# A two-layer decoder trunk: expert weights fetched in 8192-byte packets, one expert's extra columns put behind a branch, products paired

## The chip, the cores and the metric

The kernel runs on one core of one Trainium2 chip. The metric is device time in microseconds (us) from start to end of one launch. The engines are TensorE (PE: products and transposes), VectorE (DVE), ScalarE (ACT), GpSimd (POOL) and SyncE (SP), and sixteen DMA engines bring data from device memory. Each engine runs its own list of instructions in order, and semaphores tie the lists together.

## The reference, cut to what matters

256 tokens of width 1024, float32, pass two layers; after each half layer comes `x <- LayerNorm(alpha * x + sublayer(x))`.

```python
# layer 0: sliding-window attention with sinks, then a dense SwiGLU (1024 -> 3584 -> 1024)
# layer 1: sparse attention from three branches, gated and added:
kcc = gelu(flat(k blocks + pos_k) @ ck_w1) @ ck_w2     # "compressed"; the same for v
o = g0 * compressed + g1 * selected + g2 * window       # 16 heads, 4 k/v heads, 64 wide
# then the experts
vals, ids = top_k(x @ router, 2); w = softmax(vals)     # 2 of 8 for each token
for e in range(8):
    out += gate[:, e] * ((silu(x @ w_gate[e]) * (x @ w_up[e])) @ w_down[e])
```

Every expert has 3 x 1024 x 3584 float32 weights, 44.04 MB. With the reference's inputs the router gives the eight experts 60, 51, 78, 71, 71, 61, 58 and 62 (token, expert) pairs; expert 0 has 60.

## The kernel before

**Weights.** All weights pass through one planned list (`plan` L145, `plan_later` L151) as tiles of 1 MiB, 128 partitions x 8 KB. `load` (L159) issues them on SP's queue in order (L168) while a buffer is free, and each issue waits until the tile that lay in that buffer before has been used. In the expert stage there are 19 such buffers, under the names `raw`, `more` and `later`. A `w_down` tile holds 256 rows of 1024 numbers: rows 0 to 127 in the first half of each partition's 8 KB, rows 128 to 255 in the second, so a partition is filled from two places of 4 KB. The tiles of `w_gate` and `w_up` are made of pieces of 4 KB too (1024 columns), or of 2 KB for the last 512 of the 3584 columns (`WIDE` is 1024, 1024, 1024, 512).

**Dense part.** Up to the experts each weight is split into two fp32r halves (`hi` by ACT L120, `lo` by DVE L121), and each product is done three times (L204 to L206). The compression of layer 1 uses fp32 weights as they are (L803): 64 positions against 256 columns, first all of k and then all of v. The sparse attention works in units of one or two heads (`unit`, L905): scores, softmax, transposes, and then products with v (L948) that write 64 of the 128 rows of a PSUM bank, head 0 the first 64 and head 1 the others. For the second 128 tokens a unit is one head, so its four products all write the same 64 rows; for the first 128 tokens a unit has both heads, and its products alternate between them.

**Experts.** The eight experts run one after another (`run_experts`, L1162), expert 0 first and the others in an order that the kernel works out from the counts; the jobs have room for 96, 64, 96, 96, 64, 96, 96 and 64 tokens, whatever the counts are, and a leftover pass behind `tc.If(over > 0)` (L1403) takes what does not fit. The first 64 tokens of an expert are the "halves": 64 columns of PE at a time, two groups side by side (L1187 for gate and up, L1210 for down). A job with room for 96 has "quads" too: 32 tokens, four groups side by side (L1195, L1216). Both use the same weight tiles, in an order that alternates (`two`, L1168), and a group of tiles is free for new weights when both have used it. Seven of the eight experts' numbers are read by SP from the tile `whole` (L1381) before it can issue their weights. Those numbers come from the counts (`cnt`, by a product with ones, L1353 on).

The PE's order in the expert stage is the order of the code (`manual_schedule`).

Of the kernel before, what the change touches and what calls it, by code (L numbers as in the profile page):

```python
# [84 lines left out]
def trunk(ctx: ExitStack, tc: tile.TileContext, a, out, dbg=None):  # L85
# [14 lines left out]

    cbf = const.tile([P, 3 * P], BF16, name="cbf")
# [43 lines left out]
    def plan(src, exact=True, pieces=1):  # L145
        kt, cols = src.shape[0] // P, src.shape[1]
        n = max(i for i in range(1, PART // cols + 1) if kt % i == 0)
        for k0 in range(0, kt, n):
            order.append((lambda k0=k0: src[k0 * P:(k0 + n) * P, :], n, cols, exact, pieces))

    def plan_later(src, rows, cols):  # L151
# [3 lines left out]
        for r in range(rows.start, rows.stop, n * P):  # L155
            order.append((lambda r=r: src()[r:r + n * P, cols], n, width, False, 1))

    def load():

        while state["loaded"] < len(order) and len(raws) < state["ahead"]:  # L160
            src, n, cols, exact, pieces = order[state["loaded"]]
# [300 lines left out]
    plan(wa[:, :512], pieces=2)  # L462
# [21 lines left out]
    w1s = [a[w][0, q * 1024:(q + 1) * 1024, :] for w in ("b_cmp_k_w1", "b_cmp_v_w1") for q in range(2)]  # L484
# [11 lines left out]
    def plan_experts(w):  # L496

        back = None
        for wg, wu, wd in w:
            f0 = 0  # L500
            for wide in WIDE:
# [6 lines left out]
                back = wd, f, slice(0, D)  # L508
# [27 lines left out]
    with tc.tile_pool(name="swa", bufs=1) as pool:  # L536
# [53 lines left out]
        with tc.manual_schedule(engines={PE.engine}):  # L590
            for _ in project(Ts, 512, ps_q[0], 2):
                pass
# [148 lines left out]
    zeros = const.tile([P, P], BF16, name="zeros")  # L741
    POOL.memset(zeros, 0.0)
    SP.dma_start(cmask, a["cmask"].rearrange("(t p) k c -> p t k c", p=P))
    with tc.tile_pool(name="nsa", bufs=1) as pool:
# [33 lines left out]
        def compress():  # L778
# [6 lines left out]
            hc = bank().rearrange("p (k h) -> p k h", k=2)[:C]  # L785
# [20 lines left out]
            hx, hy = (pool.tile([P, 2, CMP_HID], F32, name="hx", tag="pt", bufs=PT)[:C] for _ in range(2))  # L806
# [10 lines left out]
            pb = bank().rearrange("p (k j c) -> p k j c", k=4, j=2)[:, :2, :, :]  # L817
            for k in range(2):
                for j in range(2):
                    PE.transpose(pb[:, k, j, :], hx[:, k, j * P:(j + 1) * P], ident[:C, :C])  # L820
# [82 lines left out]
        sums = {}  # L903

        def unit(t, j, heads):  # L905
# [37 lines left out]
            if heads[0] == 0:  # L943
                sums[t, j] = bank()[:, :P]
            po = sums[t, j]
# [123 lines left out]
    class Expert:  # L1069
        def __init__(self, cap, slot_e, gate_e):  # L1070

            self.cap, self.slot, self.gate = cap, slot_e, gate_e
# [89 lines left out]
    def run_experts(jobs):  # L1162
# [3 lines left out]

        state["turn"] = 0

        def two(first, second, between=None):

            steps = [first, second][::-1 if state["turn"] and second else 1]
            if second:
                state["turn"] = 1 - state["turn"]
            steps[0]()
            if between:
# [279 lines left out]
```

## Time and profile before

| | us |
|---|---|
| time, median of 3 runs | 1413.41 (1411.89 to 1418.05) |
| the profiled execution: its time | 1413.78 |
| its span in the trace | 1412.0, mean granted TensorE clock 0.99 |
| TensorE busy (matmuls) | 1360.7 (96%) |
| VectorE, ScalarE, GpSimd busy | 442.0, 342.4, 8.4 |
| DMA | 434.86 MB, mean 308 GB/s |

The busy share of TensorE hides two stages. Up to about 530 us it is the dense stage, where the DMA engines are used by half or less; from 540 us it is the expert stage, where TensorE and the DMA engines are both at or near full use. The ends of pipelined matmuls are modelled, so a stretch that reads as fully busy may hold short waits.

### The profile page before, as it was taken

How to read it: one execution, taken by the hardware profiler on the slowest of the kernel's cores; microseconds unless marked ns; L12 is line 12 of the kernel's file. 1: busy time of each engine (PE TensorE's matmuls, PEld its weight loads, DVE VectorE, ACT ScalarE, POOL GpSimd, SP SyncE). 2: the span in 40 equal slices, each digit the busy share in tenths (PEclk: the TensorE clock that was granted, in tenths of full speed). 3: DMA queues.
4: the chain of work that ended last, by engine and by line, in shares of the span. 5: the costliest groups of instructions: out<-in, count | busy, mean ns of one | idle time of the engine just before them, and what ended most of it. 6: DMA issues, size and time to landing. Idle time of an engine off the chain costs nothing. (4 is left out here: it accounts for less than half of the span.)

```text
span 1412.0 us, 23279 instructions
## 1 busy us (share of the span) xinstructions
PE 1360.7 (96%) x9761; PEld 784.5 (56%) x9762; DVE 442.0 (31%) x1004; ACT 342.4 (24%) x783; POOL 8.4 (1%) x17
## 2 busy tenths in 40 slices
PE   7999999999999999999999999999998999999984
PEld 6777888887777774453344354444343454445331
DVE  6876544556958753000101001100100100200103
ACT  5754444444456721010001001000101000100100
POOL 0000000000000000000000000000000000000000
PEclk9999999999999998999999999999999999999997
DMA  9516565554372067899999999999999999999994
GB/s 349 181 61 211 181 192 192 179 179 155 122 271 91 31 266 272 345 389 377 409 403 409 407 401 409 408 402 407 408 402 409 408 401 408 408 395 393 408 402 179
DMA packets 143679, 434.86 MB, mean 308 GB/s; under 512 B 11312, under 2 KB 18128, under 8 KB 143568
## 3 DMA queue, kind: packets, MB, share of 16 engines
q1 hardware_dynamic: 138416, 428.85, 79.3%
q10 hardware_dynamic: 5152, 4.45, 1.0%
q8 instruction: 79, 1.29, 0.4%
q14 instruction: 32, 0.26, 0.1%
HBM read 432.23 MB, written 1.05 MB: 307 GB/s over the span
## 5 line engine op out<-in xcount | busy, mean ns | idle before, releaser
L121 DVE TENSOR_TENSOR lo<-raw,hi 128x512 fp32r<-128x512 f32 (+2 forms) x244 | 166.4, 730 | 106.5 <-ACT hi L120 106.3
L1187 PE MATMUL ps<-more,Th 128*64 128x512 f32 (+1 forms) x920 | 186.8, 555 | 5.7 <-DMA more<-in_moe_w_gate 5.4
L120 ACT ACTIVATE hi<-raw 128x512 fp32r<-128x512 f32 (+2 forms) x244 | 146.0, 659 | 142.4 <-PE ps L206 129.5
L204 PE MATMUL ps<-hi,Th 128*128 128x512 f32 (+1 forms) x432 | 171.4, 397 | 4.4 <-ACT hi L120 3.2
L206 PE MATMUL ps<-hi,Tl 128*128 128x512 f32 (+1 forms) x432 | 168.6, 391 | 1.4 <-DVE Tl L121 1.4
L205 PE MATMUL ps<-lo,Th 128*128 128x512 f32 (+1 forms) x432 | 168.3, 390 | 0.0
L1244 DVE TENSOR_TENSOR h<-h,ps 128x512 f32<-128x512 f32 (+1 forms) x32 | 19.9, 621 | 448.4 <-PE ps L1187 448.4
L1187 PE MATMUL ps<-later,Th 128*64 128x512 f32 (+1 forms) x680 | 128.9, 525 | 2.1 <-DMA later<-in_moe_w_gate 1.8
L1187 PEld LDWEIGHTS ps<-more,Th 128*64 128x64 f32 x920 | 65.0, 138 | 115.5 <-issue 98.4
L204 PEld LDWEIGHTS ps<-hi,Th 128*128 128x128 f32 x432 | 81.9, 190 | 23.6 <-ACT hi L120 3.6
L1187 PE MATMUL ps<-raw,Th 128*64 128x512 f32 (+1 forms) x448 | 94.4, 561 | 0.6 <-ACT Th L1095 0.6
L1210 PE MATMUL ps<-more,hTa 128*64 128x512 f32 x408 | 92.2, 595 | 2.7 <-DMA more<-in_moe_w_down 2.7
L1236 ACT ACTIVATE h<-ps 128x512 f32<-128x512 f32 (+1 forms) x32 | 17.4, 544 | 315.1 <-PE ps L1187 315.1
L206 PEld LDWEIGHTS ps<-hi,Tl 128*128 128x128 f32 x432 | 81.8, 189 | 20.4 <-DVE Tl L121 2.9
L205 PEld LDWEIGHTS ps<-lo,Th 128*128 128x128 f32 x432 | 82.0, 190 | 16.8 <-DVE lo L121 0.4
L1187 PEld LDWEIGHTS ps<-later,Th 128*64 128x64 f32 x680 | 47.8, 137 | 72.1 <-issue 60.1
L1210 PE MATMUL ps<-later,hTa 128*64 128x512 f32 x312 | 70.3, 594 | 2.0 <-DMA later<-in_moe_w_down 2.0
L1210 PEld LDWEIGHTS ps<-more,hTa 128*64 128x64 f32 x408 | 28.4, 137 | 60.6 <-issue 54.6
L1187 PEld LDWEIGHTS ps<-raw,Th 128*64 128x64 f32 x448 | 31.7, 139 | 53.1 <-issue 48.6
L1195 PE MATMUL ps<-more,Th 128*32 128x256 f32 (+1 forms) x1136 | 60.2, 359 | 0.0
L1239 ACT ACTIVATE hb<-ps 128x256 f32<-128x256 f32 (+1 forms) x20 | 7.2, 358 | 189.0 <-PE ps L1195 189.0
L1243 DVE TENSOR_TENSOR hb<-hb,ps 128x256 f32<-128x256 f32 (+1 forms) x20 | 7.8, 388 | 142.3 <-PE ps L1195 142.3
(256 smaller groups left out, 1444.5 us busy)
## 6 DMA issues: line engine op xcount, KB each, us to landing
more<-in_moe_w_up SPq DMA_DIRECT2D x53, 1024.0 KB, 18.1
more<-in_moe_w_down SPq DMA_DIRECT2D x51, 1024.0 KB, 18.0
more<-in_moe_w_gate SPq DMA_DIRECT2D x50, 1024.0 KB, 18.2
later<-in_moe_w_down SPq DMA_DIRECT2D x38, 1024.0 KB, 15.1
later<-in_moe_w_gate SPq DMA_DIRECT2D x36, 1024.0 KB, 18.3
later<-in_moe_w_up SPq DMA_DIRECT2D x35, 1024.0 KB, 18.0
raw<-in_moe_w_gate SPq DMA_DIRECT2D x26, 1024.0 KB, 18.0
raw<-in_moe_w_up SPq DMA_DIRECT2D x24, 1024.0 KB, 18.2
```

The costliest lines, as they stand in the source:

```text
L120: state["act"] = ACT.activation(hi, src, AF.Copy)
L121: DVE.tensor_tensor(lo, src, hi.bitcast(F32), op=OP.subtract)
L204: PE.matmul(ps, xh, wh, start=first, stop=False)
L205: PE.matmul(ps, xh, wl, start=False, stop=False)
L206: PE.matmul(ps, xl, wh, start=False, stop=last)
L1187: PE.matmul(pa[h * CA:(h + 1) * CA, :wide // 2], T[:, k, :CA], parts[k // n][:, k % n, h * wide // 2:(h + 1) * wide // 2], start=k == 0, s ...
L1195: PE.matmul(pb[q * CB:(q + 1) * CB, :wide // 4].rearrange("p (b f) -> p b f", f=CB), T[:, k, CA:], w[:, q], start=k == 0, stop=k == KT - 1)
L1210: PE.matmul(ya[o * CA:(o + 1) * CA, :], hT[0][:, f % (n // 2), f // (n // 2), :], parts[f // 2][:, f % 2, o * 512:(o + 1) * 512], **ends(f))
L1236: ACT.activation(ha, ga[:, :wide // 2], AF.Silu)
L1239: ACT.activation(hb, gb[:, :wide // 4], AF.Silu)
L1243: DVE.tensor_tensor(hb, hb, ub[:, :wide // 4], op=OP.mult)
L1244: DVE.tensor_tensor(ha, ha, ua[:, :wide // 2], op=OP.mult)
```

## The change

1. **Down weights.** A tile of `w_down` of the experts is read with `(p k) f`: partition p gets the rows 2p and 2p+1, which lie next to each other in memory, so its 8192 bytes are one run. To match, the rows of the products' other operand are split by even and odd number: `Silu` and the product with `up` read PSUM with a stride of two (`paired`, `plain`), and the quads' columns are taken in the same way.
2. **Expert 0's quads behind a branch.** `beyond` is `max(count of expert 0 - 64, 0)`. PE reads it once (L1374), and each of the 12 groups of quads of job 0 (8 of gate and up, 4 of down) stands in a `tc.If(more > 0)`. The PSUM banks that they would have written are cleared by DVE. The halves come first in every group of job 0. The counts are taken earlier in the code, right after the first gather.
3. **Start.** The first weight tile comes on ACT's queue, and each of the first two in 4 pieces rather than 2. PE multiplies zeros (bf16, 512 columns) seven times ahead of the first transposes and five times behind them.
4. **Compression.** k and v are computed side by side, k in the first 64 columns of PE and v in the others, product by product; the weights come in the order k, v, k, v. What follows (gelu, transposes) works on one tile of 128 rows x 256 rather than 64 x 512.
5. **Attention of layer 1.** For the second 128 tokens the products with v of head 0 are held back until those of head 1 are ready, and then alternate with them.

```diff
@@ load
-            src = src().rearrange("(k p) f -> p k f", p=P)
+            src = src().rearrange("(p k) f -> p k f" if near else "(k p) f -> p k f", p=P)
+            queue = ACT if len(order) > 99 and state["loaded"] == 1 else SP
             for k in range(0, n, n // pieces):
-                SP.dma_start(raw[:, k:k + n // pieces, :], src[:, k:k + n // pieces, :])
+                queue.dma_start(raw[:, k:k + n // pieces, :], src[:, k:k + n // pieces, :])
...
-    plan(wa[:, :512], pieces=2)
+    plan(wa[:, :512], pieces=4)
...
-    w1s = [a[w][0, q * 1024:(q + 1) * 1024, :] for w in ("b_cmp_k_w1", "b_cmp_v_w1") for q in range(2)]
+    w1s = [a[w][0, q * 1024:(q + 1) * 1024, :] for q in range(2) for w in ("b_cmp_k_w1", "b_cmp_v_w1")]
...
-                back = wd, f, slice(0, D)
+                back = wd, f, slice(0, D), True
...
+            def turn_over(n):
+                for _ in range(n):
+                    PE.matmul(idle, zeros, zeros.unsqueeze(1).to_broadcast([P, 4, P]), start=True, stop=True)
+            turn_over(7)
+            Ts[0]
+            turn_over(5)
@@ compress
-            for k in range(2):
-                for q in range(2):
-                    (r,), = take()
-                    for i in range(8):
-                        PE.matmul(hc[:, k, :], Xs[:, k, q * 8 + i].rearrange("p g c -> p (g c)"), r[:, i, :],
-                                  start=q == 0 and i == 0, stop=q == 1 and i == 7, skip_group_check=True)
+            for q in range(2):
+                r = [w for (w,) in take(2, 1 + q)]
+                for i in range(8):
+                    for k in range(2):
+                        PE.matmul(hc[k * C:(k + 1) * C, :], Xs[:, k, q * 8 + i].rearrange("p g c -> p (g c)"),
+                                  r[k][:, i, :], start=q == 0 and i == 0, stop=q == 1 and i == 7,
+                                  skip_group_check=True)
@@ unit
-            for m, (i, br, k) in enumerate(steps):
-                h = heads[i]
-                PE.matmul(po[h * HD:(h + 1) * HD, :], v[:, k, br, g, :], pt[:, m * P:(m + 1) * P],
-                          start=k + br == 0, stop=False, skip_group_check=True)
+            held = waiting.setdefault((t, j), [])
+            held += [(k, br, heads[i], pt, m) for m, (i, br, k) in enumerate(steps)]
             if heads[-1] == 1:
+                for k, br, h, x, m in sorted(held, key=lambda e: e[:3]):
+                    PE.matmul(po[h * HD:(h + 1) * HD, :], v[:, k, br, g, :], x[:, m * P:(m + 1) * P],
+                              start=k + br == 0, stop=False, skip_group_check=True)
@@ run_experts
+            for i, step in enumerate(steps):
+                if i == 1 and ask:
+                    state["turn"] = 1
+                    x.more = x.ask() if x.more is None else x.more
+                    with tc.If(x.more > 0):
+                        step()
+                else:
+                    step()
+                if i == 0 and between:
+                    between()
...
-                ACT.activation(ha, ga[:, :wide // 2], AF.Silu)
+                ACT.activation(plain(ha, P), paired(ga[:, :wide // 2], P), AF.Silu)
...
-                DVE.tensor_tensor(ha, ha, ua[:, :wide // 2], op=OP.mult)
+                DVE.tensor_tensor(plain(ha, P), plain(ha, P), paired(ua[:, :wide // 2], P), op=OP.mult)
@@ after the first gather
+        ps = bank()[:, :NE]
+        for t in range(NT):
+            PE.matmul(ps, ones, asb[:, t, :], start=t == 0, stop=t == NT - 1)
+        DVE.tensor_copy(cnt, ps)
+        DVE.tensor_scalar(beyond, cnt[:, 0:1], -float(CA), 0.0, op0=OP.add, op1=OP.max)
...
+    experts[0].ask = lambda: nc.values_load(beyond[0:1, :], engines=[PE.engine], min_val=0, max_val=S)
```

How the instructions stand. PE at the first weight group of job 0 before: L1187 are the halves, L1195 the quads, `raw` and `more` the weight tiles.

```order
L1187 MATMUL ps<-raw,Th 64x512 [waits DMAHW3_49]
L1187 MATMUL ps<-raw,Th 64x512 x3
L1195 MATMUL ps<-raw,Th 32x256 x32
L1195 MATMUL ps<-raw,Th 32x256 [waits DMAHW4_49,PE_49]
L1195 MATMUL ps<-raw,Th 32x256 x7
L1195 MATMUL ps<-raw,Th 32x256 [waits DMAHW5_49]
```

The same place of the changed program, where L1227 are the halves, L1235 the quads, and L1205 the branch:

```order
L1227 MATMUL ps<-raw,Th 64x512 [waits DMAHW7_49]
L1227 MATMUL ps<-raw,Th 64x512 x3
L1374 TENSOR_LOAD beyond [waits DMAHW3_49,DMAHW2_49,DMAHW4_49,DMAHW1_49,DMAHW5_49,DMAHW0_49,DMAHW6_49,DVE_49,DMAHW7_49,PE_49,Activation_49]
L1374 ISA x2
L1205 COMPARE_AND_BRANCH
L1235 MATMUL ps<-raw,Th 32x256 [waits DVE_49]
L1235 MATMUL ps<-raw,Th 32x256 x31
L1205 UNCONDITIONAL_BRANCH
L1205 UNCONDITIONAL_BRANCH [waits PE_49]
L1227 MATMUL ps<-raw,Th 64x512 [waits DMAHW0_49]
```

The 32 quads now stand between a branch that can pass over them and one that rejoins; the second group's halves stand behind both, and every later group of job 0 is built the same way.

SP's queue in the changed program, from the reading of the experts' numbers (L1427) to the first down weights (L173):

```order
L173 DMA later<-in_moe_w_up 128x2x1024
L1427 TENSOR_LOAD whole [waits DMAHW3_49,DMAHW2_49,DMAHW4_49,DMAHW1_49,DMAHW5_49,DMAHW0_49,DMAHW6_49,DVE_49,DMAHW7_49,PE_49,Activation_49]
L1427 ISA x2
...
L1427 TENSOR_LOAD whole
L1427 ISA x2
L173 DMA later<-in_moe_w_down 128x2048 [waits DMAHW6_49]
L173 DMA later<-in_moe_w_down 128x2048 [waits DMAHW7_49]
L1205 UNCONDITIONAL_BRANCH
L173 DMA later<-in_moe_w_down 128x2048 [waits DMAHW0_49]
L173 DMA raw<-in_moe_w_down 128x2048 [waits DMAHW1_49,PE_49]
```

And before, the same stretch (L1381 reads the numbers, L168 are the weights):

```order
L168 DMA more<-in_moe_w_up 128x2x1024 [waits DMAHW1_49,DMAHW0_49,DVE_49]
L1381 TENSOR_LOAD whole [waits DMAHW3_49,DMAHW2_49,DMAHW4_49,DMAHW1_49,DMAHW5_49,DMAHW0_49,DMAHW6_49,DVE_49,DMAHW7_49,PE_49,Activation_49]
L1381 ISA x2
...
L1381 TENSOR_LOAD whole
L1381 ISA x2
L168 DMA later<-in_moe_w_up 128x2x1024
L168 DMA later<-in_moe_w_down 128x2x1024 [waits DMAHW2_49]
L168 DMA later<-in_moe_w_down 128x2x1024 [waits DMAHW3_49]
L168 DMA later<-in_moe_w_down 128x2x1024 [waits DMAHW4_49]
L168 DMA raw<-in_moe_w_down 128x2x1024 [waits DMAHW5_49,PE_49]
```

A down tile is one run of 2048 numbers for each partition instead of two of 1024, and at every join of PE's groups SP has a branch of its own between its issues.

## Rows read from the trace of the kernel before

**Rows 1.** The page: busy time (part 1) and DMA queues (part 3).

```profile
PE 1360.7 (96%) x9761; PEld 784.5 (56%) x9762; DVE 442.0 (31%) x1004; ACT 342.4 (24%) x783; POOL 8.4 (1%) x17
...
q1 hardware_dynamic: 138416, 428.85, 79.3%
```

**Rows 2.** Windows by stage: us, each engine's busy time, PEclk, DMA share, GB/s.

```profile
400.00:480.00 80.00, 76.14 (x512) 62.33 (x511) 62.05 (x180) 51.13 (x159) 0.00 (x0) 1.00 0.40 138
530.00:540.00 10.00, 9.42 (x28) 4.88 (x30) 6.21 (x35) 3.30 (x5) 0.00 (x0) 0.50 0.47 138
540.00:570.00 30.00, 30.00 (x282) 12.35 (x278) 4.03 (x17) 1.85 (x4) 0.00 (x0) 1.00 0.75 287
570.00:610.00 40.00, 40.00 (x340) 15.81 (x342) 2.05 (x4) 2.27 (x5) 0.00 (x0) 1.00 1.01 393
610.00:650.00 40.00, 40.00 (x488) 23.10 (x482) 3.54 (x14) 2.55 (x7) 0.00 (x0) 1.00 0.94 364
650.00:730.00 80.00, 80.00 (x448) 32.76 (x446) 8.71 (x18) 7.88 (x15) 0.00 (x0) 1.00 1.03 406
...
750.00:860.00 110.00, 110.00 (x1060) 50.88 (x1054) 10.21 (x22) 8.44 (x17) 0.00 (x0) 1.00 1.03 406
1360.00:1394.00 34.00, 26.82 (x142) 10.04 (x138) 0.42 (x1) 1.95 (x4) 0.00 (x0) 0.95 0.90 348
```

**Rows 3.** Timeline of PE at the start: start, us, line, out<-in, count.

```profile
9.39 0.79 PE L204 MATMUL ps<-hi,Th 128*128 128x512 f32 x1 [3.21 <-ACT hi L120]
...
11.14 0.63 PE L204 MATMUL ps<-hi,Th 128*128 128x512 f32 x1
...
14.66 0.40 PE L204 MATMUL ps<-hi,Th 128*128 128x512 f32 x1
...
17.24 0.39 PE L206 MATMUL ps<-hi,Tl 128*128 128x512 f32 x1
```

**Rows 4.** Windows of L803 alone, the compression's products.

```profile
389.00:406.00 17.00, 14.24 (x64) 8.60 (x64) 1.00 0.85 294
```

**Rows 5.** Timeline of PE in two units of the sparse attention.

```profile
453.74 1.09 PE L948 MATMUL ps<-pt,v 128*64 128x128 f32 x8
454.75 0.49 PE L951 MATMUL ps<-pcT,vcc 128*128 128x128 f32 x2
...
456.20 0.66 PE L948 MATMUL ps<-pt,v 128*64 128x128 f32 x8
456.79 0.49 PE L951 MATMUL ps<-pcT,vcc 128*128 128x128 f32 x2
```

**Rows 6.** DMA queues in 1035 to 1045 us (mostly 2048-byte packets).

```profile
DMA packets 1782, 3.92 MB, mean 392 GB/s; under 512 B 57, under 2 KB 57, under 8 KB 1781
...
q1 hardware_dynamic: 1781, 3.91, 104.0%
```

**Rows 7.** DMA queues in 1045 to 1055 us (4096-byte packets).

```profile
DMA packets 1069, 4.08 MB, mean 408 GB/s; under 512 B 63, under 2 KB 63, under 8 KB 1069
...
q1 hardware_dynamic: 1069, 4.08, 102.4%
```

**Rows 8.** DMA queues in 1012 to 1013 us (one packet of 8 KB).

```profile
DMA packets 107, 0.42 MB, mean 418 GB/s; under 512 B 6, under 2 KB 6, under 8 KB 106
...
q14 instruction: 1, 0.01, 2.0%
```

**Rows 9.** Windows of L1195 alone, quads of gate and up, job 0.

```profile
532.00:650.00 118.00, 25.64 (x512) 15.44 (x512) 0.97 0.89 341
```

**Rows 10.** Windows of L1216 alone, quads of down, job 0.

```profile
532.00:650.00 118.00, 10.96 (x192) 6.04 (x192) 0.97 0.89 341
```

**Rows 11.** L1381, SP's reading of the experts' numbers: ns min/median/max, first and last start.

```profile
L1381 SPq TENSOR_LOAD <-whole x7: 263/267/482, 532.9 to 536.6; - x7
```

**Rows 12.** L1403, the branch over the leftover pass: ns min/median/max, start.

```profile
L1403 PEldq COMPARE_BRANCH  x1: 3394/3394/3394, 1397.9 to 1397.9; - x1
L1403 DVEq COMPARE_BRANCH  x1: 72/72/72, 1400.1 to 1400.1; - x1
```

More of the change, by code (lines that the diff above doesn't have):

```diff
@@ L98, in bank @@
         return psum.tile([P, 512], dtype, name="ps", tag="ps")
+    zeros = const.tile([P, P], BF16, name="zeros")
+    DVE.memset(zeros, 0.0)
     cbf = const.tile([P, 3 * P], BF16, name="cbf")
@@ L148, in plan, with plan_later @@
         for k0 in range(0, kt, n):
-            order.append((lambda k0=k0: src[k0 * P:(k0 + n) * P, :], n, cols, exact, pieces))
-    def plan_later(src, rows, cols):
+            order.append((lambda k0=k0: src[k0 * P:(k0 + n) * P, :], n, cols, exact, pieces, False))
+    def plan_later(src, rows, cols, near=False):
         width = cols.stop - cols.start
@@ L155, in plan_later @@
         for r in range(rows.start, rows.stop, n * P):
-            order.append((lambda r=r: src()[r:r + n * P, cols], n, width, False, 1))
+            order.append((lambda r=r: src()[r:r + n * P, cols], n, width, False, 1, near))
     def load():
         while state["loaded"] < len(order) and len(raws) < state["ahead"]:
-            src, n, cols, exact, pieces = order[state["loaded"]]
+            src, n, cols, exact, pieces, near = order[state["loaded"]]
             state["loaded"] += 1
@@ L816, in compress @@
             yield
[L817 to L820, printed above, removed]
+            pb = bank()[:, :CMP_HID].rearrange("p (j k c) -> p k j c", j=2, k=2)
+            for j in range(2):
+                PE.transpose(pb[:, :, j, :].rearrange("p k c -> p (k c)"), hx[:, j * P:(j + 1) * P], ident)
             hk = pool.tile([P, 2, C], F32, name="hk", tag="pt", bufs=PT)
@@ L901, in compressed @@
             ACT.activation(pcT[:, :, u, :], pb, AF.Copy)
-        sums = {}
+        sums, waiting = {}, {}
         def unit(t, j, heads):
@@ L1167, in run_experts, with paired, plain, two @@
         state["turn"] = 0
-        def two(first, second, between=None):
-            steps = [first, second][::-1 if state["turn"] and second else 1]
-            if second:
-                state["turn"] = 1 - state["turn"]
-            steps[0]()
-            if between:
-                between()
-            if second:
-                steps[1]()
-        def gate_up(pa, pb, T, wide):
+        def paired(ps, n):
+            return ps.rearrange("s (m f j) -> s m j f", f=n, j=2)
+        def plain(x, n):
+            return x.rearrange("s (m j f) -> s m j f", f=n, j=2)
+        def two(x, first, second, between=None):
+            both, ask = second is not None, x.ask is not None
+            steps = [first, second][:1 + both]
+            if both and not ask:
+                if state["turn"]:
+                    steps.reverse()
+                state["turn"] = 1 - state["turn"]
+            for i, step in enumerate(steps):
[8 more added lines that the diff above has]
+                    between()
+        def cleared(ps, x):
+            if x.ask is not None:
+                DVE.memset(ps, 0.0)
+        def gate_up(pa, pb, x, wide):
+            T = x.T
+            if pb is not None:
+                cleared(pb[:, :wide // 4], x)
             parts = [w for (w,) in take(KT * wide // PART, 0)]
@@ L1192, in quarters, with down @@
                 for k in range(KT):
-                    w = parts[k // n][:, k % n].rearrange("p (b q f) -> p q b f", q=4, f=CB)
+                    w = parts[k // n][:, k % n].rearrange("p (b q f) -> p q b f", q=4, f=2 * CB)
                     for q in range(4):
-                        PE.matmul(pb[q * CB:(q + 1) * CB, :wide // 4].rearrange("p (b f) -> p b f", f=CB),
+                        PE.matmul(pb[q * CB:(q + 1) * CB, :wide // 4].rearrange("p (b f) -> p b f", f=2 * CB),
                                   T[:, k, CA:], w[:, q], start=k == 0, stop=k == KT - 1)
-            two(halves, pb is not None and quarters)
-        def down(c, hT, ya, yb, between=None):
+            two(x, halves, quarters if pb is not None else None)
+        def down(c, hT, ya, yb, x, between=None):
+            if yb is not None and c == 0:
+                cleared(yb[:, :256], x)
             n = WIDE[c] // P
@@ L1217, in quarters @@
                                   parts[f // 2][:, f % 2, q * 256:(q + 1) * 256], **ends(f))
-            two(halves, yb is not None and quarters, between)
+            two(x, halves, quarters if yb is not None else None, between)
         def finish():
@@ L1265, in back @@
                 def back(between=None, c=c, hT=hT, ys=ys, x=x):
-                    down(c, hT, *ys, between)
+                    down(c, hT, *ys, x, between)
                     if c == len(WIDE) - 1:
@@ L1335, in trunk @@
         ACT.activation(acc[t], xs[t], AF.Copy, scale=ALPHA)
-    ps = bank()
-    for t in range(NT):
-        PE.matmul(ps[:, :NE], ones, asb[:, t, :], start=t == 0, stop=t == NT - 1)
-    NR = NE - 1
-    cnt, key, rank = (moe.tile([P, NE], F32, name=x) for x in ("cnt", "key", "rank"))
+    key, rank = (moe.tile([P, NE], F32, name=x) for x in ("key", "rank"))
     is_at = moe.tile([P, NE, NE], F32, name="is_at")
```

24 lines of the change are left out of this document (12 added, 12 removed).

## Prediction

> **What bounds the kernel now.** I read the page first. TensorE is busy for 1360.7 us of a span of 1412.0, and the weight queue q1 takes 79.3% of the DMA engines [rows 1]. Neither figure says which of the two a saving must come from, so the windows by stage come next [rows 2]; the reader should look there at the columns for PE and for DMA together. From 400 to 480 us PE is busy for 76.14 of 80 us and the DMA share is 0.40: the dense part is bound by PE. From 650 us on the DMA share is 1.03 at 406 GB/s, and it is the same in 750 to 860; an expert's 44.04 MB at 406 to 408 GB/s take 108 us, and eight of them cannot go faster. PE is full too in those windows, but at 1360 to 1394, while the last weights come in, it is busy for only 26.82 of 34. So the weights set the end of the expert stage, and what counts there is how many microseconds the DMA engines lose and how fast they run.
>
> They do lose time in expert 0. Against 408 GB/s the windows give 6.6 us lost in 530 to 540 (138 GB/s), and after it 8.9 in 540 to 570 (287), 1.5 in 570 to 610 (393) and 4.3 in 610 to 650 (364), 14.7 together [rows 2]. The first loss falls where SP reads seven experts' numbers, from 532.9 to 536.6 us [rows 11], with no weight issued in between. The 14.7 come while PE runs job 0 with halves and quads and gives buffers back too slowly.
>
> The sum is made against the profiled execution, 1413.8 us, which is 0.4 above the median.
>
> **Dense part: start.** Products at the start follow each other by (14.66 - 11.14)/8 = 0.44 us at first, and by (17.24 - 14.66)/11 = 0.23 later [rows 3]. For 512 columns these are about 1.2 and 2.2 GHz, so TensorE is at its lower level until about 14 us, and it had been nearly idle until then. The zeros give it work before. If all of the eleven slow products become fast, 11 x 0.2 = 2.2 us go; pieces of 256 KB rather than 512 bring the first product perhaps 0.7 us earlier (256 KB at about 400 GB/s). I take -3; the bounds are -4.5 (the first product also finds its tile a microsecond sooner, from the second queue) and +1 (ACT spends its time on issues and the first product comes later).
>
> **Compression.** Its 64 records take 14.24 us [rows 4], all in the first 64 columns of PE. Side by side they should take half, as two heads do in the attention (below): up to -7.1. But the weights of it then have to come in half the time, and the DMA share in that stretch is 0.85 already [rows 4]. I take -5, between 0 and -7.1. The elementwise work behind it gets smaller and is left at nothing.
>
> **Products with v.** A unit with one head takes 454.75 - 453.74 = 1.01 us until the next product, a unit with both heads alternating 456.79 - 456.20 = 0.59, with eight records each [rows 5]. Of 24 units (8 pairs of heads, 3 each) sixteen have one head; paired they save 16 x 0.42 = 6.7 us. PE has 3.9 us of idle time in 80 there and DVE is busy for 62.05 [rows 2], so with a shorter PE some of it will turn into waits for softmax steps. I take -4, between 0 and -6.7. Dense together: -12. As PE sets this part, the expert stage begins that much earlier.
>
> **Down weights.** What a packet costs comes from two stretches. In 1045 to 1055 us 4.08 MB are 996 packets of 4 KB, 16 x 10 us/996 = 160.6 ns each on one engine [rows 7]. In 1035 to 1045 us, 1724 packets that are not tiny carry 3.92 MB, so some 1534 are of 2 KB and 190 of 4 KB; the former took (160 - 30.5)/1534 = 84.4 ns [rows 6]. Two packets of 2 KB thus cost 8.2 ns more than one of 4 KB. If one of 8 KB again saves 8.2 ns against two of 4 KB, a tile (128 such pairs, 8 on each engine) saves 66 ns, and 8 x 14 = 112 down tiles save 7.4 us. The one 8 KB packet that a row shows, of instructions and not of weights, takes 2.0% of 16 us, 312 to 328 ns [rows 8]; two of 4 KB at the busy share in rows 7 are 2 x 163 = 326. That is +2 to -14 ns for a pair, +2 to -13 us in all. I take -7.
>
> The trace shows a price for each packet that is still felt from 2 KB to 4 KB (84.4 ns for 2 KB is 388 GB/s, against 408). The Trainium skill, "DMA: Bandwidth & Descriptors", section "Why small descriptors are slow (HBM only)", gives about 3 cycles for each packet beside one for every 32 bytes, so 8 KB instead of 4 would be worth about 1.1%, an estimate from that page, and the term would be -3.3 us, not -7. By that rule 2 KB to 4 KB would be worth 2.3%; the trace has 5%, so I keep the row.
>
> The stride of two in PSUM touches one ACT and one DVE operation for each group; ACT is busy for 8.44 and DVE for 10.21 of 110 us there, some 0.5 us each [rows 2], while PE works on the next group. Even if each takes twice as long, it costs nothing; without that cover it would be 0.5 us for each of 32 chunks.
>
> **Branches.** With the reference's inputs expert 0 has 60 tokens, so all 12 groups of quads are passed over. They were 25.64 + 10.96 = 36.6 us of PE [rows 9, 10]. Job 0 takes 118 us before (532 to 650) and then about 81. The weights of one expert need 108, so PE waits for them, and the gain in time is not 36.6: it is what the DMA engines no longer lose. Of the 14.7 us some remains, since the buffers are full when the job begins; I take -10.5, between -5 and -14.7. The ring of buffers cannot run full in job 0 while PE has 27 us to spare there, 2.2 us for each If. The trace has two branches of this kind: 72 ns on DVE and 3394 ns on PE [rows 12]. The 3394 ns was a jump over the whole leftover pass; these skip 16 to 32 products. I take about 1 us for each, drain included, which the 2.2 us hide.
>
> The counts are now taken after the gather, so SP gets the experts' numbers some us later in relation to PE, with one more tile issued ahead (the rows of SP's order): +1.5, between 0 and +3.
>
> **Sum.** 1413.8 - 12 - 7 - 10.5 + 1.5 = 1385.8 us; with the 0.4 of the median, 1385.
>
> **Rivals.**
>
> Packets of 8 KB move like two of 4 KB. For it speaks the upper end of rows 8 (328 ns); against it the step from 2 KB to 4 KB. Time 1385 + 7 = 1392.
>
> The dense gains are half absorbed: softmax steps on DVE and the compression's weights come late. For it, DVE's 62 of 80 us and the 0.85; against it, PE's short waits. Time 1385 + 6 = 1391.
>
> The quads run all the same (count above 64): the change doesn't do what it says. Time 1385 + 10.5 = 1396.
>
> A jump costs 3.4 us, as the only one on PE did [rows 12]. Then 12 x 3.4 = 41 us stand for 36.6, job 0 takes 122 us, 4 more than before, and the DMA losses come back: 1413.4 - 12 - 7 + 1.5 + 4 = 1400.
>
> Slower: each If pays it twice, once into the block that stands for the skip and once back. 12 x 6.8 = 81 us; job 0 takes 81 + 81 = 162, 44 more than before, PE is the bound there, and the weights behind it wait for buffers: 1413.4 - 17.5 + 44 = 1440. It decides from (36.6 + 17.5)/12 = 4.5 us for an If; below that the whole is not slower. For these two speaks that the one measured jump on PE is 47 times the one on DVE; against them that what it jumped over was the code of a whole expert pass and not one group. The Trainium skill, "Runtime: NRT & Kernel Launch", section "Instruction fetch mechanics", says that a taken branch to outside the two pages that an engine holds forces a fetch of the target's page first. The 3394 ns agree with it; that a jump over 32 products stays within the two pages no run here shows.
>
> **How the numbers follow.** The forecast as it stands (its own range 1376 to 1390) has a chance of 0.62, the packets' rival 0.12, the absorbed dense gains 0.09, quads that run 0.03, a jump of 3.4 us 0.07, two of them 0.07. With all bounds at their best the sum is 1413 - 18.3 - 13 - 14.7 = 1367; with dense gains of 4, packets at +2, branches at -5 and SP at +3 it is 1409. The range 1369 to 1402 leaves out the slower rival and a little at each end. A measurement of this kernel can tell about 0.5%, 7 us, from no change. Faster by that is below 1406.3: all cases but the last two, and most of the fourth rival, 0.87; the rest of it, and prices between, give 0.06 for no change; 0.07 for slower.
>
> **What the profile after would show.** Products 0.23 us apart from the first on; 7 us of PE time in the compression and about as much again in the products with v gone, and the expert stage starting near 520 us; job 0's quads absent, PE waiting for weights in jobs 0 and 1; no window under 390 GB/s from 550 us to the end, and above 410 where down tiles move; the PE branches at well below 2.2 us. I am wrong if a branch shows more than 3 us, if the windows of job 0 still show 10 us of DMA loss, or if down tiles move at 408 GB/s.

## The result, and the profile after

The changed kernel takes 1374.35 us (median of 4 runs, 1372.94 to 1376.65) against 1413.95 before (4 runs): a ratio of 0.972 with a 95% interval of 0.969 to 0.974, some 40 us less. The forecast was 1385 in a range of 1369 to 1402. The profiled execution took 1376.65 us, 37.1 less than the one before; the terms below are compared on these two.

The page of the changed kernel, parts 1 and 3, for [rows 1]:

```profile
PE 1319.6 (96%) x9035; PEld 756.0 (55%) x9036; DVE 441.5 (32%) x1015; ACT 342.8 (25%) x783; POOL 8.2 (1%) x16
...
q1 hardware_dynamic: 123952, 427.81, 80.3%
```

PE's busy time fell by 41 us, of which the skipped quads are 36.6; the weight queue moved nearly the same bytes in 123952 packets instead of 138416. Neither line says which term gave what: that is read from the windows, the timelines and the runs below. The windows of the changed kernel around expert 0, for [rows 2] (columns as there), do:

```profile
510.00:520.00 10.00, 9.43 (x47) 5.88 (x48) 6.98 (x42) 3.41 (x5) 0.00 (x0) 0.72 0.62 227
520.00:530.00 10.00, 9.46 (x46) 3.30 (x44) 3.11 (x16) 0.87 (x2) 0.00 (x0) 1.00 0.69 262
530.00:540.00 10.00, 9.85 (x48) 3.81 (x49) 1.62 (x5) 1.36 (x3) 0.00 (x0) 1.00 1.01 411
540.00:560.00 20.00, 19.24 (x91) 6.92 (x88) 1.92 (x5) 0.32 (x2) 0.00 (x0) 1.00 1.03 412
560.00:600.00 40.00, 38.91 (x234) 19.22 (x233) 3.98 (x16) 3.49 (x10) 0.00 (x0) 1.00 1.02 405
600.00:640.00 40.00, 33.13 (x144) 10.42 (x142) 7.03 (x12) 4.58 (x8) 0.00 (x0) 1.00 1.02 413
640.00:700.00 60.00, 49.54 (x276) 18.88 (x272) 1.85 (x6) 3.40 (x7) 0.00 (x0) 1.00 1.02 408
```

Against 408 GB/s, 510 to 530 us lose 8.0 us, where SP waits for the experts' numbers and reads them; from 530 on next to nothing is lost. Before, 6.6 us were lost at that point and another 14.7 in job 0 [rows 2]. PE now has idle time at 600 to 700 us, 17.3 of 100: it waits for weights there, as forecast.

SP's readings in the changed kernel, for [rows 11] (ns min/median/max, first and last start):

```profile
L1427 SPq TENSOR_LOAD <-whole x7: 265/268/469, 517.5 to 521.5; - x7
...
L1427 SPq EVENT_SEMAPHORE  x5: 28/28/3702, 513.5 to 517.4; - x5
```

They begin 15 us earlier than before and take as long. Ahead of them SP stood for 3.7 us (the semaphore of 3702 ns, 0.99 us in the kernel before), until DVE had written the numbers; so not all of the 8.0 us belong to the readings. PE's branches around the quads (L1205) and the one over the leftover pass (L1449), for [rows 12]:

```profile
L1205 PEldq COMPARE_BRANCH  x12: 207/235/1153, 519.3 to 614.2; - x12
...
L1449 PEldq COMPARE_BRANCH  x1: 3397/3397/3397, 1359.5 to 1359.5; - x1
```

The twelve branches took 0.2 us in the middle and 1.2 at most, while the jump over the leftover pass took 3.4 us as before. That is the time of the branch instruction alone. At each join PE also waits until its own products are done (`[waits PE_49]` in the order of the changed program), as the second join shows:

```profile
527.59 1.92 PE L1227 MATMUL ps<-more,Th 128*64 128x512 f32 x8
529.88 7.09 PE L1227 MATMUL ps<-more,Th 128*64 128x512 f32 x32 [0.38 <-PEq L1205]
```

The products of the halves start in pairs, one pair each 0.43 us, and the last pair ahead of this join started at 528.88. So the next pair came 1.00 us after it, 0.57 late. Over the first eleven joins 0.33 to 0.57 us are lost each, some 5 us with the twelfth.

The start in the changed kernel, PE's timeline, for [rows 3]:

```profile
1.03 3.17 PE L600 MATMUL ps<-zeros 128*128 128x512 bf16 x7 [1.03 <-DVE zeros L102]
5.42 2.12 PE L229 MATMUL ps<-cf,x 128*128 128x128 f32 x8 [1.22 <-DMA x<-in_x]
7.33 2.34 PE L600 MATMUL ps<-zeros 128*128 128x512 bf16 x5
9.11 0.99 PE L209 MATMUL ps<-hi,Th 128*128 128x512 f32 x1
...
10.59 0.39 PE L209 MATMUL ps<-hi,Th 128*128 128x512 f32 x1
...
15.23 0.40 PE L211 MATMUL ps<-hi,Tl 128*128 128x512 f32 x1
```

Products are 0.23 us apart from the fourth on, and the 24th starts at 15.23 instead of 17.24. The first starts at 9.11, hardly sooner than before (9.39): the transposes of x (L229) wait for x until 5.42 (4.24 before), and the five products of zeros stand between their end and the first product.

In this execution nothing of these 2 us is left at 65 us, in the first attention. In a second execution of the same kernel (`changed_again`, below) the same product starts 1.6 us sooner. It is the 145th of these products, shown for the kernel before, the changed one and its repeat:

```profile
64.98 0.50 PE L204 MATMUL ps<-hi,Th 128*128 128x512 f32 x1
...
64.95 0.50 PE L209 MATMUL ps<-hi,Th 128*128 128x512 f32 x1
...
63.35 0.50 PE L209 MATMUL ps<-hi,Th 128*128 128x512 f32 x1
```

Windows of that attention in the changed kernel (columns PE, PEld, DVE, ACT, POOL, PEclk, DMA share, GB/s after the length):

```profile
50.00:55.00 5.00, 2.86 (x24) 2.40 (x23) 4.90 (x18) 5.00 (x18) 0.00 (x0) 0.98 0.17 53
55.00:60.00 5.00, 5.00 (x25) 4.38 (x25) 4.55 (x18) 3.38 (x11) 0.00 (x0) 0.50 0.00 0
```

And in its repeat:

```profile
50.00:55.00 5.00, 3.73 (x28) 2.94 (x26) 4.83 (x19) 4.91 (x17) 0.00 (x0) 1.00 0.41 146
55.00:60.00 5.00, 3.99 (x36) 3.35 (x36) 5.00 (x20) 4.63 (x16) 0.00 (x0) 1.00 0.00 0
```

DVE and ACT are busy for 3.4 to 5 of every 5 us in both. What differs is the granted clock: in the first execution PE was busy for 2.86 of 5 us, and for the next 5 us the clock was 0.50, its lower level; in the repeat it stayed at 1.00.

The compression and what follows it. DVE's timeline of the gelu in the kernel before:

```profile
406.59 0.68 DVE L808 TENSOR_TENSOR hx<-hx 64x512 f32<-64x512 f32 x1 [12.30 <-ACT hx L807]
...
410.30 3.34 DVE L814 RECIPROCAL hx<-hx 64x512 f32<-64x512 f32 x1
...
413.87 0.67 DVE L815 TENSOR_TENSOR hx<-hx 64x512 f32<-64x512 f32 x1
```

The same three of its seven steps in the changed kernel:

```profile
399.49 0.43 DVE L822 TENSOR_TENSOR hx<-hx 128x256 f32<-128x256 f32 x1 [5.13 <-ACT hx L821]
...
401.85 1.75 DVE L828 RECIPROCAL hx<-hx 128x256 f32<-128x256 f32 x1
...
403.82 0.41 DVE L829 TENSOR_TENSOR hx<-hx 128x256 f32<-128x256 f32 x1
```

The chain of seven steps took 7.95 us (406.59 to 414.54) and takes 4.74, with 256 numbers for each partition instead of 512; the reciprocal alone went from 3.34 to 1.75 us. The products themselves, L816 now, take half:

```profile
L816 PE MATMUL ps<-raw,X x64: 379/379/430, 389.8 to 398.6; 128*64 128x256 f32 x64
```

They start at 389.8 as before, and the last at 398.6 instead of 405.5.

The products with v, PE's timeline of the changed kernel, for [rows 5]:

```profile
433.72 1.09 PE L964 MATMUL ps<-pt,v 128*64 128x128 f32 x16
434.74 0.49 PE L966 MATMUL ps<-pcT,vcc 128*128 128x128 f32 x2
```

Sixteen records for both heads take 1.02 us until the next product, as long as eight for one head did [rows 5].

### The profile page after: what moved, and what is told of

It is laid out like the page before. It is cut to its first block, busy times and chain, and to the rows that moved or that the text cites. A ratio compares the mean times of both kernels' runs of the same rounds, so it can differ in the third digit from the quotient of the medians.

```text
span 1374.8 us, 21889 instructions
## 1 busy us (share of the span) xinstructions
PE 1319.6 (96%) x9035; PEld 756.0 (55%) x9036; DVE 441.5 (32%) x1015; ACT 342.8 (25%) x783; POOL 8.2 (1%) x16
## 3 DMA queue, kind: packets, MB, share of 16 engines
q1 hardware_dynamic: 123952, 427.81, 80.3%
## 5 line engine op out<-in xcount | busy, mean ns | idle before, releaser
L1227 PE MATMUL ps<-more,Th 128*64 128x512 f32 (+1 forms) x920 | 188.3, 557 | 4.1 <-DMA more<-in_moe_w_up 2.3
L1227 PE MATMUL ps<-later,Th 128*64 128x512 f32 (+1 forms) x680 | 129.4, 526 | 3.3 <-DMA later<-in_moe_w_up 2.1
L1227 PEld LDWEIGHTS ps<-more,Th 128*64 128x64 f32 x920 | 65.3, 138 | 114.9 <-issue 96.3
L1227 PE MATMUL ps<-raw,Th 128*64 128x512 f32 (+1 forms) x448 | 91.5, 551 | 3.0 <-DMA raw<-in_moe_w_gate 2.5
L1227 PEld LDWEIGHTS ps<-later,Th 128*64 128x64 f32 x680 | 47.5, 137 | 75.4 <-issue 60.3
L1227 PEld LDWEIGHTS ps<-raw,Th 128*64 128x64 f32 x448 | 31.4, 137 | 55.6 <-issue 44.3
L1235 PE MATMUL ps<-more,Th 128*32 128x256 f32 (+1 forms) x928 | 50.3, 364 | 4.2 <-DMA more<-in_moe_w_gate 4.2
L1252 PEld LDWEIGHTS ps<-later,hTa 128*64 128x64 f32 x312 | 22.1, 137 | 49.2 <-issue 40.8
```

The costliest lines, as they stand in the source:

```text
L1227: PE.matmul(pa[h * CA:(h + 1) * CA, :wide // 2], T[:, k, :CA], parts[k // n][:, k % n, h * wide // 2:(h + 1) * wide // 2], start=k == 0, s ...
L1235: PE.matmul(pb[q * CB:(q + 1) * CB, :wide // 4].rearrange("p (b f) -> p b f", f=2 * CB), T[:, k, CA:], w[:, q], start=k == 0, stop=k == KT ...
L1252: PE.matmul(ya[o * CA:(o + 1) * CA, :], hT[0][:, f % (n // 2), f // (n // 2), :], parts[f // 2][:, f % 2, o * 512:(o + 1) * 512], **ends(f))
```

## The experiments

All were timed in 5 rounds beside the kernel before, and each ratio is to it: 1417.7 us beside `no_pair`, `dense_alone`, `changed_again` and `late_old_start`, 1413.8 beside the others. Differences are against the changed kernel's 1374.35, for `no_pair`, `dense_alone` and `late_old_start` against its repeat on the same chip (1373.32).

**The packets.** `no_near`, the changed kernel with down weights as before:

```diff
-                back = wd, f, slice(0, D), True
+                back = wd, f, slice(0, D)
...
-            return ps.rearrange("s (m f j) -> s m j f", f=n, j=2)
+            return ps
...
```

> The changed kernel with the down weights fetched as before: two runs of 4096 bytes for each partition, and no stride of two behind it. Theory (a packet has a price that falls on the weight queue): 112 tiles x 8 pairs x 8.2 ns, so 5 to 8 us slower than the changed kernel, about 1381, and every down tile lands at 408 GB/s again. Rival (the packets are worth nothing, and the queue is steadier only because job 0 no longer holds it up): within 1.5 us of the changed kernel, about 1374. Second rival (the strided reads cost PE time): faster than the changed kernel.

1380.51 us (ratio to before 0.975, 0.972 to 0.978): 6.2 slower. `near_alone` is the kernel before with this part alone:

> The kernel before with the down weights in runs of 8192 bytes alone (and the stride of two behind them), nothing else changed. Theory (a packet's price counts wherever the weights set the end, and job 0's losses stay): 5 to 7 us faster than the kernel before, about 1407.5. Rival (with quads in job 0 faster weights only fill the ring sooner and more is lost in job 0): 0 to 3 us faster, about 1412.

1407.39 us (ratio 0.995, 0.994 to 0.997): 6.4 faster. The two agree from either side, so the packets have a price of their own, whether job 0 stalls or not. A window of the changed kernel (770 to 780 us) in which most bytes come in large packets, for [rows 7]:

```profile
DMA packets 698, 4.17 MB, mean 417 GB/s; under 512 B 63, under 2 KB 63, under 8 KB 257
```

417 GB/s instead of 408. In the traces down tiles land 2.50 us apart in the middle in both kernels with the large packets, and 2.56 without them (before, `no_near`): 60 ns less, against the 66 of the working.

**The branch.** `no_branch`, with the quads of expert 0 always computed:

```diff
-    experts[0].ask = lambda: nc.values_load(beyond[0:1, :], engines=[PE.engine], min_val=0, max_val=S)
+    experts[0].ask = None
```

> The changed kernel with the quads of expert 0 computed always, in turns with the halves as before; all else stays. Theory (the branch gives the DMA engines back what they lost in job 0): 11 to 15 us slower than the changed kernel, about 1387, and the windows between 520 and 640 us fall under 300 GB/s in places again. Rival (the losses went because the expert stage begins sooner and the packets are larger): at most 4 us slower, about 1378, with no such windows. The 36.6 us of PE time themselves would give 1411, which neither theory expects.

1385.12 us (0.978, 0.975 to 0.981): 10.8 slower, just under the 11 to 15 that were expected. Its windows:

```profile
540.00:560.00 20.00, 20.00 (x190) 8.31 (x188) 1.55 (x3) 1.58 (x3) 0.00 (x0) 1.00 0.87 341
560.00:600.00 40.00, 40.00 (x378) 16.60 (x376) 1.55 (x3) 1.56 (x3) 0.00 (x0) 1.00 0.99 387
600.00:640.00 40.00, 40.00 (x398) 21.46 (x396) 2.46 (x11) 3.43 (x9) 0.00 (x0) 1.00 0.94 369
```

PE is full and the weights lose 3.3, 2.1 and 3.8 us in these three, 9.2 together, which the changed kernel does not. At 510 to 530 us they lose 9.8, against 8.0, so the windows account for some 11. The windows under 300 GB/s that were expected between 520 and 640 us are not there; the losses are spread. That the gain is not PE time is shown by putting PE time back. `pad27` adds products of zeros ahead of each of the eight branches around gate and up quads:

```diff
...
+                    for _ in range(27 if pad is not None else 0):
+                        PE.matmul(pad[:, :256], zeros, zeros.unsqueeze(1).to_broadcast([P, 2, P]), start=True,
+                                  stop=True, skip_group_check=True)
                     with tc.If(x.more > 0):
...
```

> The changed kernel with 27 products of zeros of 256 columns (2.9 us at full clock) ahead of each of the 8 branches around gate and up quads of expert 0: 23 us of work more for PE in job 0. Theory (PE waits for weights in jobs 0 and 1, so some 25 us of PE time there are free): at most 4 us slower than the changed kernel, about 1376. Rival (PE is still on the path in job 0, and the gain of the branch is PE time): 15 to 23 us slower, about 1393.

1380.73 us (0.976, 0.975 to 0.978): 6.4 slower, between the two theories. `pad60` has 60 of them:

> As the run with 27 products of zeros, with 60 (6.4 us each, 51 us in all, about what twice the one far jump of the kernel before would cost for each branch). Theory (the cover of some 25 us is used up, and the rest of the time holds up the buffers): 15 to 30 us slower than the changed kernel, about 1396, still faster than the kernel before. Rival (the cover is larger, as job 1 waits for weights too): under 10 us slower, about 1382. Second rival (no cover): 45 to 51 us slower, about 1422.

1407.67 us (0.995, 0.993 to 0.997): 33 slower, just past the theory's 30 and outside both rivals (under 10, 45 to 51). Windows of `pad27`:

```profile
540.00:560.00 20.00, 19.55 (x120) 9.88 (x118) 2.10 (x5) 1.58 (x3) 0.00 (x0) 1.00 0.88 327
...
600.00:640.00 40.00, 38.94 (x221) 17.63 (x220) 5.21 (x12) 4.53 (x9) 0.00 (x0) 1.00 1.02 410
640.00:700.00 60.00, 58.74 (x324) 25.04 (x320) 4.92 (x11) 4.60 (x9) 0.00 (x0) 1.00 1.02 409
```

And of `pad60`:

```profile
540.00:560.00 20.00, 19.48 (x131) 11.61 (x130) 1.41 (x4) 1.58 (x3) 0.00 (x0) 1.00 0.70 255
560.00:600.00 40.00, 39.25 (x243) 20.77 (x240) 2.18 (x6) 1.58 (x3) 0.00 (x0) 1.00 0.83 322
600.00:640.00 40.00, 39.18 (x322) 29.33 (x321) 3.99 (x16) 2.56 (x7) 0.00 (x0) 1.00 0.80 307
640.00:700.00 60.00, 59.39 (x278) 21.81 (x276) 7.31 (x13) 5.76 (x10) 0.00 (x0) 1.00 0.90 361
```

With 23 us of work more, PE's idle time at 600 to 700 fell from 17.3 to 2.3 us, and 4 us of weights were lost at 540 to 560 (327 GB/s): some 17 us lay beside the weights, and 6 did not. So the cover (what PE can do more without costing time) is about 17 us in these two jobs, not 27; the joins take some 5 of the difference, and the rest is not explained by a run. With 51 us, 33 came through, 51 - 18, and weights are lost from 540 to 700, 33 us against 408 GB/s in the four windows.

**Products with v.** `no_hold`:

```diff
...
+            for m, (i, br, k) in enumerate(steps):
+                h = heads[i]
+                PE.matmul(po[h * HD:(h + 1) * HD, :], v[:, k, br, g, :], pt[:, m * P:(m + 1) * P],
+                          start=k + br == 0, stop=False, skip_group_check=True)
...
-            held = waiting.setdefault((t, j), [])
-            held += [(k, br, heads[i], pt, m) for m, (i, br, k) in enumerate(steps)]
...
```

> The changed kernel with the products with v of the second 128 tokens done unit by unit as before, not held and not alternating. Theory (side by side they cost half, and the later products also spare PE the wait for the copy out of PSUM): 9 to 12 us slower, about 1385. Rival (only the pairing counts): 5 to 7 us slower, about 1380, with PE's waits in that stretch unchanged at about 1 us.

1384.59 us (0.978, 0.975 to 0.980): 10.2 slower, the theory's time. Its trace bears out the rival's mechanism: the stretch is 8.5 us longer than in the changed kernel's, PE's waits in it are 0.8 us against 1.0, and the shorter products alone are worth 8.0 (worked out below). So by the trace it is the pairing, at a higher price than the rival gave it; the other 1.7 of the 10.2 us are not explained by it.

**Start.** `old_start` has no zeros, and the first tile in two pieces on SP's queue:

```diff
-            queue = ACT if len(order) > 99 and state["loaded"] == 1 else SP
+            queue = SP
...
-    plan(wa[:, :512], pieces=4)
+    plan(wa[:, :512], pieces=2)
...
-            turn_over(7)
...
-            turn_over(5)
```

> The changed kernel with the start as before: no products of zeros, two pieces of 512 KB for the first tile, all on SP's queue. Theory (the 2 us won by the 24th product are lost again in the first attention, which VectorE and ScalarE bound): within 1 us of the changed kernel, about 1374. Rival (they were lost only in the profiled execution, whose clock fell to the lower level at 66 us, and other executions keep them): 2 to 3 us slower, about 1377.

1373.63 us (0.970, 0.968 to 0.973): no difference that can be told. The clock of the profiled execution fell at 54.8 us on the axis used here, not at 66. The time is the theory's, but the traces do not bear out its reason, that DVE and ACT take the 2 us back. From the first product to the 145th, the four traces with the old start (before, `near_alone`, `old_start`, `late_old_start`) have 55.3 to 56.0 us, all with a granted clock of 1.00 at 50 to 65 us. The ten with the new start fall into three groups by that clock: 52.8 to 53.3 us in the three at 1.00, 54.0 to 55.1 in the six at 0.89, and 55.8 in the one at 0.77, the profiled execution above. So the gain outlasts the attention where the clock stays up, and a lower clock there takes part of it or all. And the first product itself starts no sooner, at 8.8 to 10.7 us with the new start and at 7.7 to 9.4 with the old one. What is left is too small for these times, as the runs of one kernel differ by 4. No run has the zeros alone, so what makes the clock fall with the new start is not shown.

**Compression.** `no_pair` puts it back as before (k, then v, one tile of 64 x 512 behind it):

```diff
...
-            for q in range(2):
-                r = [w for (w,) in take(2, 1 + q)]
-                for i in range(8):
-                    for k in range(2):
...
+            for k in range(2):
+                for q in range(2):
+                    (r,), = take()
+                    for i in range(8):
...
-            hx, hy = (pool.tile([P, CMP_HID], F32, name="hx", tag="pt", bufs=PT) for _ in range(2))
+            hx, hy = (pool.tile([P, 2, CMP_HID], F32, name="hx", tag="pt", bufs=PT)[:C] for _ in range(2))
...
```

> The changed kernel with the compression as before: k first and then v, all in the first 64 columns of PE, weights in the order k, k, v, v. Theory (this stretch is bound by PE): 6 to 8 us slower than the changed kernel, about 1381. Rival (the weights of it arrive no faster, and part of the gain lies in waits elsewhere): 2 to 4 us slower, about 1377.

1385.14 us (0.979, 0.976 to 0.982): 11.8 slower than the repeat beside it (1373.32), above both. Its trace has 6.9 us of that in the products, and 4.6 more behind them, where PE stands once for 2.8:

```profile
421.24 3.61 PE L396 MATMUL ps<-cf,kd 128*128 128x128 f32 x16 [2.80 <-ACT kd L122]
```

This wait is in the trace of before too (at 421.87), and not in that of the changed kernel. Some 1.1 of the 4.6 us are this execution's own: the granted clock was 0.50 at 422 to 425 us, and these sixteen records took 3.61 us, against 2.65 in the trace of before, where 3.4 us more than in the changed kernel lie behind the products. PE waits for `kd`, the keys that DVE rotates and ACT splits, not for the gelu's result; `kd` stands behind the gelu in the queues of DVE and ACT. ACT ahead of `kd`, in the kernel before and in the changed one:

```profile
419.11 2.19 ACT L120 ACTIVATE hi<-raw 128x512 fp32r<-128x512 f32 x4 [1.18 <-PE ps L206]
...
408.79 2.19 ACT L122 ACTIVATE hi<-raw 128x512 fp32r<-128x512 f32 x4 [1.05 <-issue]
```

Before, these four splits could start only when PE's products had ended; in the changed kernel PE had 2.7 us of products left when they started. The order of ACT's work is not the same either: before, a copy and four splits more stand ahead of `kd`. No run has the paired products with the old tile behind them, so how the 3.4 us divide between the smaller steps and this order is not shown.

**Do the parts add up?** `dense_alone` has neither the packets nor the branch (both edits above together).

> The changed kernel without the larger packets and without the branch: what stays are the start, the compression, the products with v held back, and the counts taken earlier. Theory (the parts add up, since each undone alone cost 6.2 and 10.8 us): 1374.4 + 17 = 1391. Rival (the two help each other: large packets are worth more where job 0 no longer stalls, or the branch more where tiles come faster): 1395 or more, the dense part's 19 us off the kernel before. Second rival (they overlap, each taking what the other would): under 1388.

1391.17 us (0.982, 0.979 to 0.984): 17.9 above the repeat beside it, 6.2 + 10.8 = 17.0 by the single runs. The parts add up.

**SP's readings.** `late_numbers` gives each reading a place of its own:

```diff
...
+    def who_at(place):
+        if place not in who:
+            who[place] = numbered[0](place)
+        return who[place]
...
-                            a[name][0, bass.ds(who[place], 1)].rearrange("a r c -> (a r) c"))
+                            a[name][0, bass.ds(who_at(place), 1)].rearrange("a r c -> (a r) c"))
...
```

> The changed kernel with SP's seven readings of the experts' numbers moved: each stands right ahead of that expert's first weight rather than all seven ahead of expert 0's first down weights. Theory (the weights set the end from the first tile of expert 0 on, so each microsecond that SP's queue gives back there comes off the end): the windows from 510 to 530 us lose some 6 us against 408 GB/s in the changed kernel, of which 4 to 6 come back, about 1369. Rival (buffers, not SP, hold the weights back there): within 1.5 us of the changed kernel, about 1374. Second rival (each reading now breaks a full queue later): slower.

1372.06 us (0.971, 0.969 to 0.973): 2.3 faster, between the theory (5) and the rival (1.5), and inside what the runs of one kernel differ by. Then, on one chip, the changed kernel again and `late_old_start`, the late readings with the old start:

> The changed kernel once more, to stand beside the others on one chip. Every theory: 1373 to 1376. What it tells is whether the kernel with late readings and the old start, run beside it, is faster by more than the runs differ.

It took 1373.32 us (0.969, 0.967 to 0.972).

> The changed kernel with SP's seven readings each ahead of its expert's first weight, and the start as before (no products of zeros, all on SP's queue in pieces of 512 KB). Theory (the readings give back 2 to 4 us, the start nothing): 1370 to 1372, 2 to 5 us below the changed kernel on the same chip. Rival (the late readings' gain was noise): within 1.5 us of it.

It took 1373.34 us (0.970, 0.967 to 0.972): nothing between them. Windows of the repeat around SP's readings:

```profile
510.00:520.00 10.00, 10.00 (x45) 5.23 (x45) 7.25 (x45) 3.42 (x5) 0.00 (x0) 0.71 0.59 213
520.00:530.00 10.00, 9.54 (x46) 3.44 (x44) 2.31 (x10) 0.87 (x2) 0.00 (x0) 1.00 0.89 342
530.00:540.00 10.00, 9.85 (x50) 3.73 (x47) 0.79 (x3) 1.36 (x3) 0.00 (x0) 1.00 1.01 408
```

Of `late_numbers`:

```profile
510.00:520.00 10.00, 9.53 (x52) 4.08 (x52) 8.26 (x52) 4.29 (x7) 0.00 (x0) 1.00 0.82 312
520.00:530.00 10.00, 9.70 (x46) 3.68 (x44) 2.23 (x7) 0.00 (x0) 0.00 (x0) 1.00 1.00 410
530.00:540.00 10.00, 9.85 (x48) 3.54 (x46) 0.00 (x0) 1.36 (x3) 0.00 (x0) 1.00 1.01 390
```

Over the three windows the repeat loses 6.4 us against 408 GB/s, `late_numbers` 2.7 and `late_old_start` 5.1. In these windows moving the readings gives microseconds back; in `late_old_start` 1.7 of them are lost again at 530 to 540 (337 GB/s). Whether 2 us remain in the end is not settled: the runs of one kernel differ by 4. No version was found that is clearly faster than the changed kernel.

## Why the prediction came out as it did

| term | forecast | measured |
|---|---|---|
| start | -3 | 0 (trace), +0.7 (`old_start`), inside the scatter |
| compression and gelu | -5 | -10.3 (trace), -11.8 (`no_pair`) |
| products with v | -4 | -8.5 (trace), -10.2 (`no_hold`) |
| packets | -7 | -6.2 and -6.4 (`no_near`, `near_alone`) |
| branch, with the counts moved | -10.5 + 1.5 | -10.8 (`no_branch`, counts stay moved) |
| sum | -28 | -37.1 (profiled executions), -39.6 (medians) |

In the first three lines "trace" compares the start of the same product in the two traces, ahead of and behind each part. No run puts the counts back, so the +1.5 was not measured by itself.

The forecast lay 11 us high, and 6.8 of it are the dense part: -12 where the trace has -18.8. None of the three signs of being wrong came. **Right** were that the weights set the end of the expert stage, so that 36.6 us of skipped work are worth only what the weights lost in job 0; that PE would wait for weights in jobs 0 and 1; and the price of a packet, 8.2 ns, extrapolated from 2 KB and 4 KB to 8 KB. The estimate from the Trainium skill's rule ("DMA: Bandwidth & Descriptors", "Why small descriptors are slow (HBM only)") was -3.3 for it; the runs have twice that.

**The start was wrong** in two steps. That the pieces "bring the first product perhaps 0.7 us earlier" failed: its weights were split at 4.59 us instead of 9.34, but x came 1.2 us later and the zeros stood in front of it. And "the expert stage begins that much earlier" failed for the rest: the faster products came, and then the clock fell in the first attention in seven of ten traces with this start and took part of the gain or all. The working had no term for a lower clock behind the start.

**The compression was mis-sized** by two terms. I took -5 for the products out of fear that the weights would come late; they started at the same 389.8 and took half, -6.9. And I set a term to nothing: "the elementwise work behind it gets smaller and is left at nothing". Behind the products 3.4 us went: the gelu's seven steps became 3.2 us shorter, and PE's wait of 2.8 for `kd` went with the time that stands behind them on DVE and ACT. That the shorter steps alone ended the wait is argued and not shown.

**The products with v were mis-sized** in two ways. The most that pairing could give I put at 6.7 us, from eight alternating records in 0.59 us; sixteen take 1.02, so it is 8 x (2 x 1.01 - 1.02) = 8.0. And I cut the bound to 4 for waits on softmax steps, reading the 3.9 us of idle time in 400 to 480 us as such. Most of it was another wait, the one for `kd`, as the list of PE's waits in that stretch shows (us in total, times, longest):

```profile
PE ps L391 <- ACT kd L120: 2.8, 1, 2.8
PE ps L948 <- ACT pt L941: 0.8, 1, 0.8
```

In the attention itself PE waited 0.8 us before and 1.0 in the changed kernel: no gain turned into waits.

**The branch** met its sum, and partly by luck. The working had 14.7 us to win and left some of it in place; in the changed kernel without the branch there were about 11 (9.2 of them in job 0), and next to nothing remained. The cover for PE is 17 us and not 27, and an If costs PE 0.3 to 0.6 us with its drain where I took about 1. The rival that a jump costs 3.4 us fell with the 0.2 us of the branch rows. Its page's rule ("Runtime: NRT & Kernel Launch", "Instruction fetch mechanics", of the Trainium skill) speaks of targets outside the pages that are held, and these short jumps show no such stall, while the far one of the same trace took 3.4 us again. What the slower rival's price, 81 us in all, would have done can be estimated from `pad60`: with 18 us of cover 63 remain, and 1374 + 63 = 1437 is near that rival's 1440.

## What to carry to other kernels

Where transfers set the end, work that is taken from the engine beside them is worth what the transfers lose in that stretch, and no more; adding dummy work back in two sizes shows how large the cover is. Where an engine sets the end, look at what it waits for next as well: what went behind the halved products was worth half as much as they were. Before idle time is used as a bound, ask which instruction it stands ahead of: 2.8 of the 3.9 us here belonged to another part. And before a small gain is called gone or kept, compare more than one trace: in two executions of the same kernel the same product started 1.6 us apart.

## What the runs showed of the hardware

- A branch instruction on PE that skips 16 to 32 products took 0.2 us (median of 12), where the jump over the leftover pass took 3.4 in both kernels [rows 12]. With the drain at the join PE lost 0.3 to 0.6 us each time.
- In a window with mostly 8 KB packets from device memory the rate was 417 GB/s, with 4 KB packets 408, and with 2 KB packets about 388 by the working from [rows 6].
- After a stretch of 5 us in which PE was busy for 2.86, the granted clock was 0.50 for the next 5 us in one execution; in `old_start`, busy for 2.75, it stayed at 1.00. From the 25th product to the 145th the new start took 45.4 us where the clock stayed at 1.00 at 50 to 65 us, 46.4 to 46.6 where it was 0.89, and 48.0 where it was 0.77.
